# Hybrid decoder block on one core: earlier decay rows and a narrower join in the DeltaNet solve

## The chip, the cores and the metric

The kernel runs on one core of a Trainium2 chip. The metric is the device time of one execution in microseconds, as the median of three runs. The core has TensorE (PE; its weight loads are listed as PEld), VectorE (DVE), ScalarE (ACT), GpSimd (POOL) and SyncE (SP), which here issues nearly all transfers from one queue, in order.

## The reference

One layer over 4096 tokens of width 1024, all in float32:

```python
h = rms_norm(x, attn_norm)
proj = h @ w_in                       # q, k, v, gate, beta, alpha of group A; q, k, v, gate of group B
o_a = gated_delta_net(...)            # 4 heads of 128, chunked WY form, decay exp(cumsum(g))
o_b = retention(...)                  # 4 heads of 128, rotary phase, fixed decay per head
x = x + concat(o_a, o_b) @ w_out
x = x + hierarchical_moe(rms_norm(x, ffn_norm), ...)   # 64 experts, top group, top 2
return rms_norm(x, final_norm)
```

The change touches `gated_delta_net` alone. For each chunk it forms a strictly lower triangular matrix from k, beta and the decay, and solves a unit triangular system with it:

```python
a_mat = where(strict, (kb @ k.T) * decay, 0)
uw = triangular_solve(a_mat, [v*beta, kb*exp(gc)], lower=True, unit_diagonal=True)
```

## The kernel before

The mixer (both attention groups) takes tokens in eight blocks of 512 and chunks of 128. A block has four stages in the order a1, b1, a0, b0: `a` projects for two DeltaNet heads (a *pair*), `b` for two retention heads. A stage `a` has four "normal" projections (`proj_n`, L244 to L246; 128 tokens by 256 columns, 24 matmuls) for the gates and three groups of two "transposed" ones (`proj_t`, L232 to L234) for q, k and v; a stage `b` has sixteen normal ones. Each matrix is split into a high and a low part, hence three matmuls per step. The results go into one of two accumulators in PSUM (`pacc`), and a projection can't start before the one two back has been emptied: by L846 and L849 (rotary phase, VectorE), L861 (ScalarE) or L277 and L279 (gates).

Everything else is laid between the projections by hand. After each projection, and in the middle of each transposed one, `unit` is called. It first issues the stores that are due, then runs the steps that `STEPS` lists: `W` asks for the four weight tiles of the next group (`wq`, 512 KB each, only at the group's first unit), `E` empties the accumulator, `L` advances the DeltaNet chain of the pair, and so on. A group of four units counts `u` from 0 to 3. The chain `gdn_pair` is a generator: `PLAN[pr]` says how many of its steps each unit runs. It is started at the end of a stage `a` and runs through the following stages `b` and `a`. In each block the pair `pr` = 1 comes first (called the first pair here), `pr` = 0 second.

The steps of `gdn_pair` that matter here:

- At its start it asks for `E` (L641): for each of two heads the running decays of 512 tokens, repeated over 128 partitions, read from `gcd` in DRAM, which L380 wrote during the first projection pair of stage a1. Then come transposes and norms; `decay` (L653 to L658) makes the decay matrix from `E`: an exponential on ScalarE, a product on GpSimd, four operations on VectorE, another exponential.
- L696 to L704 form the matrices `at` and `am`. L711 and L712 take the diagonal 32-blocks, a constant pattern is loaded into `V` (L686), and L722 to L732 solve the 32-blocks on VectorE. L736 clears `X2`; L739 and L756 turn the result back.
- The join of 32-blocks into 64-blocks: `mask` (L749) multiplies `at` by a 0/1 mask on GpSimd, for each head; L784 multiplies the masked matrix with `X`, ScalarE copies all 512 columns (L785), L791 multiplies with `U`, VectorE adds (L792).
- The join of 64-blocks into 128 (L765 to L778) works on 64 by 64 pieces.
- L801 to L826 run over the chunks; each ends in `norm_out`, which leaves a store of `mx` (two buffers) to `mixed` in the list of stores (L296).

After the mixer come the output projection, the routing and the experts, which the change leaves alone.

Of the kernel before, what the change touches and what calls it, by code (L numbers as in the profile page):

```python
# [8 lines left out]
F32 = mybir.dt.float32  # L9
# [3 lines left out]
AF = mybir.ActivationFunctionType  # L13
OP = mybir.AluOpType
# [3 lines left out]
P = 128  # L18
# [3 lines left out]
NT = T // P  # L22
# [4 lines left out]
GA, BA = 1536, 2048  # L27
QB, KB, VB, GB = 2056, 2568, 3080, 3592
NEXP, NGRP, EPG, DE = 64, 8, 8, 256
LEVELS = (32, 64)  # L30
B = LEVELS[0]
NB = P // B
NQ = P // (2 * NB * NT)

C_UT, C_NEG, C_LV = 0, 128, 256
C_CV = C_LV + 128 * len(LEVELS)
C_EF = C_CV + 4
C_ID = C_EF + 4
C_ROW = C_ID + P
# [3 lines left out]
def constants(S):  # L43
    i = np.arange(P)
    J, I = np.meshgrid(i, i, indexing="ij")
    c = np.zeros((P, C_N), np.float64)
    c[:, C_ID:C_ID + P] = J == I
    c[:, C_UT:C_UT + P] = I >= J
    c[:, C_ROW:] = (I[:, :B // NQ, None] * NQ + J[:, :B // NQ, None] % B // (2 * NT) == i[:B]).reshape(P, -1)
    c[:, C_NEG:C_NEG + P] = np.where(I >= J, 0.0, -1e4)  # L50
    for n, m in enumerate(LEVELS):
        c[:, C_LV + n * P:C_LV + (n + 1) * P] = (
            (J // (2 * m) == I // (2 * m)) & ((J // m) % 2 == 0) & ((I // m) % 2 == 1))
    for h in range(4):
        g = 1.0 - 2.0 ** (-5.0 - h)
        c[:, C_CV + h] = DK ** -0.5 * g ** -(i + 1.0)
        c[:, C_EF + h] = EPS * g ** (-2.0 * (i + 1.0))
    pos = np.arange(S, dtype=np.float32)
    inv = (np.float32(10000.0) ** (-np.arange(0, DK, 2, dtype=np.float32) / np.float32(DK))).astype(np.float32)
    ang = (pos[:, None] * inv[None, :]).astype(np.float32).astype(np.float64)  # L60
    co, si = np.cos(ang), np.sin(ang)
    rope = np.concatenate([co, -si, si], axis=1).astype(np.float32)
    return c.astype(np.float32), rope


def rows(ap, off, pat):
    return bass.AP(tensor=ap.tensor, offset=ap.offset + off, ap=pat)
# [6 lines left out]
def mixer(tc, outer, banks, x, attn_norm, w_in, conv_a, a_log, dt_bias, norm_a, norm_b, cst, rope, mixed, clear, w_out, x1, wsp):  # L74


    nc = tc.nc
# [3 lines left out]
    pacc, ptr, psm = (pool(tc, banks, n, b, space=PSUM) for n, b in (("pa", 2), ("pt", 3), ("ps", 3)))  # L81
    wp, hp, xp = (pool(tc, outer, n, 1) for n in "whx")
    with ExitStack() as ctx:
        cp, gp, sp = (pool(tc, ctx, n, b, side="right") for n, b in (("c", 1), ("g", 2), ("s", 2)))
# [4 lines left out]
        C = cp.tile([P, C_ID], F32, name="cst")  # L89
        ident = wp.tile([P, P], F32, name="id")  # L90
# [102 lines left out]
        la, lb = Lane(), Lane()  # L193
        late, bg, stores = [], [], []
# [7 lines left out]
            if bg:  # L202
                bg.pop(0)()

        def store():
            due, stores[:] = stores[:], []
            for f in due:
                f()

# [1 line left out]

        def unit(u, evac, kind):

            store()
            g = gi[0]
            act = dict(L=la.tick, E=evac or (lambda: None), T=later, S=lambda: ahead(4 * g + 5, u, False),
                       W=lambda: ahead(4 * g + 5, u, True), B=behind)
            for o in STEPS[kind]:
                act[o]()
            if u == 3:  # L220
                gi[0] += 1

        def w(k):
            m = 4 * gi[0] + k // 2
# [58 lines left out]
        def norm_out(po, e, gs, t0, col):  # L283
            ss = sp.tile([P, 2], F32, name="ss", bufs=4)
            jk = sp.tile([P, P], BF, name="jk", bufs=2)
            for i in range(2):
                nc.scalar.activation(jk, po[:, i], AF.Square, accum_out=ss[:, i:i + 1])
            nc.vector.scalar_tensor_tensor(ss, ss, 1.0 / P, e, op0=OP.mult, op1=OP.add)  # L288
            nc.gpsimd.tensor_tensor(ss, ss, ex[:, 0:2], op=OP.pow)  # L289
            m = sp.tile([P, 2, P], F32, name="mx", bufs=2)  # L290

            def rest():
                for i in range(2):
                    nc.vector.scalar_tensor_tensor(m[:, i], po[:, i], ss[:, i:i + 1], gs[:, i * P:i * P + P],
                                                   op0=OP.mult, op1=OP.mult)
                stores.append(lambda: nc.sync.dma_start(mixed[t0:t0 + P, col:col + 256], m.rearrange("p a b -> p (a b)")))  # L296
            return rest
# [40 lines left out]
        def decays(ba):  # L338
# [41 lines left out]
            nc.sync.dma_start(gcd, gr)  # L380
            yield gcd

        L = dict(locals())
        with tc.manual_schedule():
            x_load(0)
# [41 lines left out]
            for sb in range(NS):  # L427
# [4 lines left out]
                for kind, pr in stages:  # L432
# [3 lines left out]
                    if kind == "a":  # L436

                        n = 264 if pr else 256
                        gs = []
                        if pr:  # L440
                            ba = gp.tile([P, NT, 8], F32, name="ba")
                        for i in range(NT):
# [4 lines left out]
                            a = proj_n(i, n)  # L447
# [6 lines left out]
                        if pr:  # L454
                            dec = decays(ba)
                            co = next(dec)
                            bg += [lambda: next(dec)] + [lambda: None] * 1 + [lambda: next(dec), lambda: box.append(next(dec))]
                            box = []


                        dst, ready = [], []
                        for wi in range(3):
                            dst.append(gp.tile([P, 2, T], F32, name="qkv"[wi] + "t", bufs=(1, 2, 1)[wi]))
                            for cc in range(2):
                                ch = wi * 4 + 2 * pr + cc
                                a = proj_t(cc)
                                unit(2 * cc + 1, lambda: take(a, ch, dst[wi][:, cc], ready), "t")
                        la.start(gdn_pair(tc, sb, pr, co, box[0], gs, dst, ready, L), PLAN[pr])
                    else:
                        if last and pr and sb:  # L470
                            out.begin()
# [149 lines left out]
                      zt[:, None, :].to_broadcast([P, m, ZW]))  # L621


def gdn_pair(tc, sb, pr, co, gcd, gs, qkv, ready, L):
    nc = tc.nc
    sp, gp, ptr, psm, ex, Sa = L["sp"], L["gp"], L["ptr"], L["psm"], L["ex"], L["Sa"]
    ident, neg, C, norm_out = L["ident"], L["neg"], L["C"], L["norm_out"]
# [7 lines left out]
    vr = gp.tile([P, 2, NT, P], F32, name="vr", bufs=1)  # L635
    jk = sp.tile([P, P], BF, name="jk", bufs=2)
    tkc = lambda w, i, c: tk[:, w, 4 * i + c:4 * i + c + 1]
    E, qd = [], []
    for i, h in enumerate(hs):
        e = gp.tile([P, NT, P], F32, name="E", bufs=2)  # L640
        nc.sync.dma_start(e, rows(gcd, h * P, [[0, P], [4 * P, NT], [1, P]]))  # L641
        E.append(e)

    def turn(src):
        tr = ptr.tile([P, NT, P], F32, name="tr")
# [35 lines left out]
    at, am = [], []  # L681
    blocks = [(slice(b * B, b * B + B), b) for b in range(NB)]
    at2, N = (gp.tile([P, 2 * NT, P], F32, name=n, bufs=1) for n in ("at", "U"))
    N = N.rearrange("p a b -> p (a b)").rearrange("p (r s) -> p r s", r=B)
    V = sp.tile([P, B // NQ, B], F32, name="V", bufs=1)
    nc.sync.dma_start(V.rearrange("p r s -> p (r s)"), L["cst"][:, C_ROW:])  # L686
    for i, h in enumerate(hs):
        a_ = at2[:, i * NT:i * NT + NT]
        m_ = gp.tile([P, NT, P], F32, name="am")
# [47 lines left out]
    yield  # L737
    for sl, b in blocks:
        nc.vector.transpose(X2[sl, :, sl].rearrange("p c (r q) -> p r q c", q=NQ), V[sl])  # L739
    U, X = ([t[:, :NT], t[:, NT:]] for t in (U2, X2))  # L740
    flat = lambda t: t.rearrange("p a b -> p (a b)")
    mts = {}

    def mask(li):
        lv = C[:, C_LV + li * P:C_LV + li * P + P][:, None, :].to_broadcast([P, NT, P])
        mts[li] = []
        for i in range(2):
            mt = gp.tile([P, NT, P], F32, name="E", bufs=2)
            nc.gpsimd.tensor_tensor(mt, at[i], lv, op=OP.mult)  # L749
            mts[li].append(mt)  # L750

    mask(0)
    yield

    for i in range(2):
        nc.vector.transpose(flat(U[i]), flat(X[i]))  # L756
    yield
    for li, m in enumerate(LEVELS):
        if m == 64:

            a, b = slice(0, 64), slice(64, P)
            for i in range(2):
                tr = ptr.tile([P, NT, P], F32, name="tr")
                for c in range(NT):
                    nc.tensor.transpose(tr[a, c, a], U[i][a, c, a], ident[a, a])  # L765
                nc.scalar.activation(X[i][a, :, a], tr[a, :, a], AF.Copy)
            yield
            for i in range(2):
                w = psm.tile([P, NT, P], F32, name="sm")
                for c in range(NT):  # L770
                    nc.tensor.matmul(w[b, c, a], at[i][a, c, b], X[i][a, c, a], start=True, stop=True)
                nc.scalar.activation(X[i][b, :, a], w[b, :, a], AF.Copy)
            yield
            for i in range(2):
                pu = psm.tile([P, NT, P], F32, name="sm")
                for c in range(NT):
                    nc.tensor.matmul(pu[a, c, b], X[i][b, c, a], U[i][b, c, b], start=True, stop=True)
                nc.vector.tensor_tensor(U[i][a, :, b], U[i][a, :, b], pu[a, :, b], op=OP.add)  # L778
            yield
            continue  # L780
        for i in range(2):
            w = psm.tile([P, NT, P], F32, name="sm")
            for c in range(NT):
                nc.tensor.matmul(w[:, c], mts[li][i][:, c], X[i][:, c], start=True, stop=True)  # L784
            nc.scalar.activation(X[i], w, AF.Copy)  # L785
        yield
        r = s = slice(0, P)
        for i in range(2):
            pu = psm.tile([P, NT, P], F32, name="sm")
            for c in range(NT):  # L790
                nc.tensor.matmul(pu[r, c, s], X[i][:, c, r], U[i][:, c, s], start=True, stop=True)  # L791
            nc.vector.tensor_tensor(U[i][r, :, s], U[i][r, :, s], pu[r, :, s], op=OP.add)  # L792
        yield


    rest = None
# [1014 lines left out]
```

## Time and profile before

| what | us |
|---|---|
| median of three runs | 3616.17 (3609.36 to 3617.98) |
| the profiled execution | 3614.18 |
| its span, first to last instruction | 3612.4 |
| TensorE busy in it | 3405.1 (94%) |
| VectorE, ScalarE, GpSimd busy | 2206.6, 1500.5, 1052.1 |

The profile lists instructions by their line in the kernel. "Idle before" is the time an engine stood before an instruction, with what ended the wait; "issue" is time in which it waited for nothing that the profile shows. A matmul of float32 operands is two instructions. The granted clock (PEclk) is the share of TensorE's full 2.4 GHz; 0.50 is 1.2 GHz.

### The profile page before, as it was taken

What the parts mean: (1) busy time and instruction counts of PE and PEld (TensorE: products, weight loads), DVE (VectorE), ACT (ScalarE), POOL (GpSimd) and SP (SyncE); (2) the same over time, 40 slices, a digit from 0 to 9 for tenths busy, and PEclk for the clock granted to TensorE, in tenths of its full rate; (3) what the DMA queues carried; (4) which work ended last, traced back from release to release, by engine and by line L of the source; (5) the groups of instructions that cost most, each with busy time, mean ns of one, the idle gap of its engine ahead of it and who ended that gap; (6) DMA issues with size and microseconds to landing.
All of it is one profiled execution on the core that took longest, in us unless ns stands there. A gap on an engine that the chain in (4) does not pass through costs nothing. (4 is left out here: it accounts for less than half of the span.)

```text
span 3612.4 us, 65017 instructions
## 1 busy us (share of the span) xinstructions
PE 3405.1 (94%) x24177; PEld 3118.7 (86%) x24177; DVE 2206.6 (61%) x5766; ACT 1500.5 (42%) x3322; POOL 1052.1 (29%) x1352
## 2 busy tenths in 40 slices
PE   7999999999999999999999999999969999999996
PEld 6988988988998998989899898888858888888885
DVE  6785565575576566466466564444456777777775
ACT  4343233233233333323323332222136666776775
POOL 1322222232232232232222220211223444444443
PEclk9999999999999999999999999999979999999998
DMA  8766346445455355364444435332268898899996
GB/s 269 239 209 216 125 144 208 147 145 189 147 158 191 127 173 187 140 187 162 159 146 172 161 110 168 115 121 97 78 198 287 286 307 291 304 327 331 342 317 194
DMA packets 463375, 711.10 MB, mean 197 GB/s; under 512 B 151329, under 2 KB 342353, under 8 KB 463057
## 3 DMA queue, kind: packets, MB, share of 16 engines
q1 hardware_dynamic: 426688, 622.16, 51.9%
q0 software_dynamic: 34976, 84.20, 6.6%
q8 instruction: 191, 3.13, 0.3%
q14 instruction: 128, 1.04, 0.1%
q10 hardware_dynamic: 1392, 0.56, 0.1%
HBM read 606.32 MB, written 131.99 MB: 204 GB/s over the span
## 5 line engine op out<-in xcount | busy, mean ns | idle before, releaser
L244 PE MATMUL acc<-wq,hh 128*128 128x256 f32 (+1 forms) x2560 | 760.1, 297 | 92.8 <-issue 51.4
L245 PE MATMUL acc<-wq,hh 128*128 128x256 f32 (+1 forms) x2560 | 733.5, 287 | 1.9 <-DVE wq L150 1.9
L246 PE MATMUL acc<-wq,hl 128*128 128x256 f32 (+1 forms) x2560 | 733.0, 286 | 2.1 <-DVE hl L324 2.1
L244 PEld LDWEIGHTS acc<-wq,hh 128*128 128x128 f32 x2560 | 495.6, 194 | 104.4 <-issue 63.9
L245 PEld LDWEIGHTS acc<-wq,hh 128*128 128x128 f32 x2560 | 496.7, 194 | 2.4 <-DVE wq L150 2.4
L246 PEld LDWEIGHTS acc<-wq,hl 128*128 128x128 f32 x2560 | 495.1, 193 | 2.8 <-DVE hl L324 2.8
L232 PE MATMUL acc<-hh,wq 128*128 128x512 f32 x768 | 317.8, 414 | 0.5 <-DMA wq<-wsp 0.3
L234 PE MATMUL acc<-hh,wq 128*128 128x512 f32 x768 | 302.1, 393 | 0.0
L233 PE MATMUL acc<-hl,wq 128*128 128x512 f32 x768 | 300.9, 392 | 0.0
L1622 PEld LDWEIGHTS g<-xT,gu 128*128 128x128 f32 x2048 | 273.3, 193 | 15.0 <-DVE xT L1554 5.4
L1622 PE MATMUL g<-xT,gu 128*128 128x128 f32 (+30 forms) x2048 | 279.0, 295 | 2.7 <-DVE xT L1554 2.7
L1622 PE MATMUL u<-xT,gu 128*128 128x128 f32 (+30 forms) x2048 | 275.9, 293 | 0.0
L1622 PEld LDWEIGHTS u<-xT,gu 128*128 128x128 f32 x2048 | 266.3, 191 | 1.9
L272 DVE SCALAR_TENSOR_TENSOR cv<-xin,pcol,cv 128x512 f32<-128x512 f32 x288 | 216.3, 751 | 73.3 <-ACT cv L270 66.5
L280 POOL TENSOR_TENSOR gs<-gs,nrow 128x256 f32<-128x256 f32 x128 | 97.4, 761 | 512.6 <-DVE gs L279 486.9
L850 POOL TENSOR_TENSOR rqk<-rqk,rb 128x256 f32<-128x256 f32 x128 | 116.1, 908 | 250.8 <-DVE rb L849 178.3
L1597 POOL DMA_INDIRECT out_dram<-xg,mi x100 | 131.8, 1318 | 188.0 <-DVE ss L1593 95.9
L976 PE MATMUL y<-dh,hh 128*128 128x512 f32 (+16 forms) x400 | 164.7, 412 | 20.5 <-ACT ys L1565 12.8
L1565 ACT ACTIVATE ys<-y,mf 128x512 f32<-128x512 f32 (+22 forms) x200 | 133.6, 679 | 114.2 <-PE y L978 95.6
L1568 POOL DMA_INDIRECT xg<-out_dram,mi x97 | 100.3, 1034 | 251.6 <-PE tr L1552 45.3
L234 PEld LDWEIGHTS acc<-hh,wq 128*128 128x128 f32 x768 | 144.2, 188 | 32.9
L289 POOL TENSOR_TENSOR ss<-ss,ex 128x2 f32<-128x2 f32 x128 | 101.7, 795 | 238.3 <-DVE ss L288 205.2
(376 smaller groups left out, 8007.1 us busy)
## 6 DMA issues: line engine op xcount, KB each, us to landing
wq<-wsp SPq DMA_DIRECT2D x420, 512.0 KB
gu<-in_w_gate_dram SPq DMA_DIRECT2D x128, 512.0 KB
gu<-in_w_up_dram SPq DMA_DIRECT2D x128, 512.0 KB
dn<-in_w_down_dram SPq DMA_DIRECT2D x64, 1024.0 KB
xi<-in_x_dram SPq DMA_DIRECT2D x64, 512.0 KB
wsp<-wq SPq DMA_DIRECT2D x60, 512.0 KB
mixed<-mx SPq DMA_DIRECT2D x128, 128.0 KB
out_dram<-zt SPq DMA_DIRECT2D x8, 2048.0 KB
```

The source lines that it names most:

```text
L232: nc.tensor.matmul(a, wh[:, s], hh[:, k, :], start=(k == 0), stop=False)
L233: nc.tensor.matmul(a, wh[:, s], hl[:, k, :], start=False, stop=False)
L234: nc.tensor.matmul(a, wl[:, s], hh[:, k, :], start=False, stop=(k == KC - 1))
L244: nc.tensor.matmul(a[:, :n], hh[:, k, s], wh[:, :n], start=(k == 0), stop=False)
L245: nc.tensor.matmul(a[:, :n], hh[:, k, s], wl[:, :n], start=False, stop=False)
L246: nc.tensor.matmul(a[:, :n], hl[:, k, s], wh[:, :n], start=False, stop=(k == KC - 1))
L272: nc.vector.scalar_tensor_tensor(cv, xin[:, j:j + T], tap(j), cv, op0=OP.mult, op1=OP.add)
L850: nc.gpsimd.tensor_tensor(o.rearrange("p h s d -> p (h s d)"), o.rearrange("p h s d -> p (h s d)"), b.rearrange("p h s d -> p (h s d)"), o ...
L976: nc.tensor.matmul(out, a.hi, b.hi, start=(i == 0), stop=False)
L1565: nc.scalar.activation(self.y[:R, s], y[:R], AF.Copy, scale=self.f[:R, WT, self.n:self.n + 1])
L1597: so = nc.gpsimd.indirect_dma_start(out=orow, out_offset=self.idx(0), in_=self.xg[:self.G], in_offset=None, bounds_check=S - 1, oob_is_err ...
L1622: nc.tensor.matmul(o[:, b, :R], self.w.gu[k // 4][:, k % 4, i * DE + b * P:i * DE + b * P + P], self.xT[:, k, :R], start=(k == 0), stop=(k ...
```

## The change

Three edits, in the functions shown above.

- The request for `E` and `V` moves from the chain into a new function `preload`, which stage `a` calls before the third pair of transposed projections (`wi` = 2). `E` is no longer used for masks.
- The join of 32-blocks multiplies without masks, and with 64 moving columns in place of 128; all eight chunks of a pair of heads go into one PSUM tile. The rows that matter are copied (ScalarE, 32 rows by 256 columns, two copies) in place of whole tiles and in place of additions on VectorE. In the 64-join the two heads share a PSUM tile and a copy. The number of steps of the chain is the same.
- In a group's first three units the stores that are due are issued after the unit's steps, and so behind the weight loads; in the fourth they stay in front. `mx` has three buffers.

```diff
-        def store():
-            due, stores[:] = stores[:], []
+        def store(n=None):
+            due, stores[:n] = stores[:n], []
...
-            store()
+            due = len(stores)
+            if u == 3:
+                store()
...
             if u == 3:
                 gi[0] += 1
+            else:
+                store(due)
...
-            m = sp.tile([P, 2, P], F32, name="mx", bufs=2)
+            m = sp.tile([P, 2, P], F32, name="mx", bufs=3)
...
+        def preload(pr, gcd):
+
+            E = []
+            for h in (2 * pr, 2 * pr + 1):
+                e = gp.tile([P, NT, P], F32, name="E", bufs=2)
+                nc.sync.dma_start(e, rows(gcd, h * P, [[0, P], [4 * P, NT], [1, P]]))
+                E.append(e)
+            V = sp.tile([P, B // NQ, B], F32, name="V", bufs=1)
+            nc.sync.dma_start(V.rearrange("p r s -> p (r s)"), cst[:, C_ROW:])
+            return E, V
...
                             for cc in range(2):
+                                if wi == 2 and cc == 0:
+                                    first = preload(pr, box[0])
                                 ch = wi * 4 + 2 * pr + cc
...
-                        la.start(gdn_pair(tc, sb, pr, co, box[0], gs, dst, ready, L), PLAN[pr])
+                        la.start(gdn_pair(tc, sb, pr, co, first, gs, dst, ready, L), PLAN[pr])
...
-    mask(0)
-    yield
-
-    for i in range(2):
-        nc.vector.transpose(flat(U[i]), flat(X[i]))
-    yield
...
-        for i in range(2):
-            w = psm.tile([P, NT, P], F32, name="sm")
-            for c in range(NT):
-                nc.tensor.matmul(w[:, c], mts[li][i][:, c], X[i][:, c], start=True, stop=True)
-            nc.scalar.activation(X[i], w, AF.Copy)
-        yield
-        r = s = slice(0, P)
-        for i in range(2):
-            pu = psm.tile([P, NT, P], F32, name="sm")
-            for c in range(NT):
-                nc.tensor.matmul(pu[r, c, s], X[i][:, c, r], U[i][:, c, s], start=True, stop=True)
-            nc.vector.tensor_tensor(U[i][r, :, s], U[i][r, :, s], pu[r, :, s], op=OP.add)
-        yield
+    U = [U2[:, :NT], U2[:, NT:]]
+    yield
+
+    for t in range(2):
+        h = slice(t * NT, t * NT + NT)
+        nc.vector.transpose(U2[:, h].rearrange("p a b -> p (a b)"), X2[:, h].rearrange("p a b -> p (a b)"))
+    yield
+    even, odd = (lambda t, c, o=o: t[:, c].rearrange("p (m o s) -> p m o s", o=2, s=B)[:, :, o] for o in range(2))
+    w = psm.tile([P, 2 * NT, 2 * B], F32, name="sm")
+    for c in range(2 * NT):
+        nc.tensor.matmul(w[:, c], at2[:, c], even(X2, c), start=True, stop=True)
+    for m in range(2):
+        r = slice((2 * m + 1) * B, (2 * m + 2) * B)
+        nc.scalar.activation(X2[r, :, 2 * m * B:2 * m * B + B], w[r, :, m * B:m * B + B], AF.Copy)
+    yield
+    pu = psm.tile([P, 2 * NT, 2 * B], F32, name="sm")
+    for c in range(2 * NT):
+        nc.tensor.matmul(pu[:, c], X2[:, c], odd(U2, c), start=True, stop=True)
+    for m in range(2):
+        r = slice(2 * m * B, 2 * m * B + B)
+        nc.scalar.activation(U2[r, :, (2 * m + 1) * B:(2 * m + 2) * B], pu[r, :, m * B:m * B + B], AF.Copy)
+    yield
+    a, b = slice(0, 64), slice(64, P)
+    tr = ptr.tile([P, 2 * NT, 64], F32, name="tr")
+    for c in range(2 * NT):
+        nc.tensor.transpose(tr[a, c], U2[a, c, a], ident[a, a])
+    nc.scalar.activation(X2[a, :, a], tr[a], AF.Copy)
+    yield
...
+        nc.tensor.matmul(pu[a, c], X2[b, c, a], U2[b, c, b], start=True, stop=True)
+    nc.vector.tensor_copy(U2[a, :, b], pu[a])
+    yield
```

## Rows read from the trace of the kernel before

**Rows 1.** Busy time by stretch: us; PE, PEld, DVE, ACT, POOL; PEclk, DMA share, GB/s.
```profile
1060.00:1145.00 85.00, 85.00 (x605) 77.94 (x604) 46.08 (x122) 34.25 (x112) 18.41 (x35) 1.00 0.63 200
0.00:2135.00 2135.00, 2022.00 (x14845) 1900.47 (x14846) 1325.27 (x3658) 740.51 (x2207) 567.46 (x836) 0.98 0.52 172
```

**Rows 2.** Groups by line and shape, TensorE, mixer: busy us, mean ns; idle before.
```profile
L244 PE MATMUL acc<-wq,hh 128*128 128x256 f32 x2304 | 681.9, 296 | 90.4 <-issue 51.4 <-DVE gs L279 21.6 <-DVE rb L849 13.5
...
L232 PE MATMUL acc<-hh,wq 128*128 128x512 f32 x768 | 317.8, 414 | 0.5 <-DMA wq<-wsp 0.3
```

**Rows 3.** Waits, whole span: who waited for whom, us, times, longest.
```profile
DVE E L657 <- ACT qd L653: 81.3, 16, 6.6
...
ACT qd L653 <- DMA E<-gcd: 58.0, 14, 5.0
```

**Rows 4.** Timeline of a second pair, 1005 to 1053 us: start, duration, engine, line.
```profile
1009.46 0.63 ACT L653 ACTIVATE qd<-E 128x512 f32<-128x512 f32 x1 [3.77 <-DMA E<-gcd]
...
1013.95 0.48 DVE L849 TENSOR_TENSOR rb<-acc,rt 128x128 f32<-128x128 f32 x2
...
1014.53 0.36 PE L244 MATMUL acc<-wq,hh 128*128 128x256 f32 x1 [3.30 <-issue]
...
1027.56 0.36 PE L244 MATMUL acc<-wq,hh 128*128 128x256 f32 x1 [0.93 <-DVE rb L849]
...
1052.82 0.58 PE L244 MATMUL acc<-wq,hh 128*128 128x256 f32 x1 [2.46 <-DVE gs L279]
```

**Rows 5.** Busy time by stretch, after the two stalls of that pair.
```profile
1015.20:1018.60 3.40, 3.40 (x18) 3.40 (x17) 3.40 (x7) 0.00 (x0) 3.02 (x4) 0.50 0.04 7
...
1052.90:1056.30 3.40, 3.40 (x17) 3.40 (x18) 1.90 (x4) 1.32 (x3) 1.41 (x2) 0.52 0.03 12
1056.40:1059.80 3.40, 3.40 (x32) 3.40 (x31) 0.92 (x3) 1.43 (x6) 1.38 (x3) 1.00 0.00 0
```

**Rows 6.** Timeline of SP's queue before a first pair, 1115 to 1140 us.
```profile
1115.73 0.32 SPq L296 DMA_DIRECT2D mixed<-mx  x1
1116.14 1.82 SPq L143 DMA_DIRECT2D wq<-wsp  x4
1125.70 10.85 SPq L296 DMA_DIRECT2D mixed<-mx  x2
1136.67 2.08 SPq L143 DMA_DIRECT2D wq<-wsp  x4
1138.85 1.15 SPq L641 DMA_DIRECT2D E<-gcd  x2
```

**Rows 7.** Busy time by stretch, around that request; DMA share and GB/s last.
```profile
1124.00:1136.00 12.00, 12.00 (x83) 10.99 (x82) 7.86 (x17) 5.33 (x16) 2.09 (x4) 1.00 0.03 11
1138.00:1148.00 10.00, 9.62 (x84) 9.43 (x82) 1.93 (x5) 4.39 (x20) 1.11 (x2) 1.00 0.96 334
```

**Rows 8.** Timelines of VectorE and GpSimd: the 32-block solve and the masks.
```profile
240.00 5.00 DVE L726 SCALAR_TENSOR_TENSOR V<-U,V 128x31 f32<-128x31 f32 x12
...
1033.74 2.60 POOL L749 TENSOR_TENSOR E<-at,cst 128x512 f32<-128x512 f32 x2
...
1168.22 2.59 DVE L726 SCALAR_TENSOR_TENSOR V<-U,V 128x31 f32<-128x31 f32 x12
...
2085.64 5.10 DVE L726 SCALAR_TENSOR_TENSOR V<-U,V 128x31 f32<-128x31 f32 x12
```

**Rows 9.** Timelines of TensorE and its weight loads: joins and two narrow matmuls.
```profile
1072.82 1.95 PE L791 MATMUL sm<-U,X 128*128 128x128 f32 x16
...
1083.45 1.14 PE L771 MATMUL sm<-X,at 64*64 64x64 f32 x16
...
1099.45 0.30 PEld L366 LDWEIGHTS sm<-co,cst 128*128 128x128 f32 x2
1099.67 0.30 PEld L367 LDWEIGHTS sm<-co,cst 128*128 128x128 f32 x2
```

**Rows 10.** Groups by line and shape, ScalarE, mixer.
```profile
L711 ACT ACTIVATE X<-at 32x256 f32<-32x256 f32 x64 | 26.6, 415 | 30.1 <-DVE at L702 29.6
```

More of the change, by code (lines that the diff above doesn't have):

```diff
@@ L29 @@
 NEXP, NGRP, EPG, DE = 64, 8, 8, 256
-LEVELS = (32, 64)
-B = LEVELS[0]
+B = 32
 NB = P // B
 NQ = P // (2 * NB * NT)
-C_UT, C_NEG, C_LV = 0, 128, 256
-C_CV = C_LV + 128 * len(LEVELS)
+C_UT, C_NEG, C_CV = 0, 128, 256
 C_EF = C_CV + 4
@@ L50, in constants @@
     c[:, C_NEG:C_NEG + P] = np.where(I >= J, 0.0, -1e4)
-    for n, m in enumerate(LEVELS):
-        c[:, C_LV + n * P:C_LV + (n + 1) * P] = (
-            (J // (2 * m) == I // (2 * m)) & ((J // m) % 2 == 0) & ((I // m) % 2 == 1))
     for h in range(4):
@@ L621, in zero, with gdn_pair @@
                       zt[:, None, :].to_broadcast([P, m, ZW]))
-def gdn_pair(tc, sb, pr, co, gcd, gs, qkv, ready, L):
+def gdn_pair(tc, sb, pr, co, first, gs, qkv, ready, L):
     nc = tc.nc
@@ L637, in gdn_pair @@
     tkc = lambda w, i, c: tk[:, w, 4 * i + c:4 * i + c + 1]
[L638 to L642, printed above, removed]
+    (E, V), qd = first, []
     def turn(src):
@@ L684, in gdn_pair @@
     N = N.rearrange("p a b -> p (a b)").rearrange("p (r s) -> p r s", r=B)
-    V = sp.tile([P, B // NQ, B], F32, name="V", bufs=1)
-    nc.sync.dma_start(V.rearrange("p r s -> p (r s)"), L["cst"][:, C_ROW:])
     for i, h in enumerate(hs):
@@ L739, in gdn_pair @@
         nc.vector.transpose(X2[sl, :, sl].rearrange("p c (r q) -> p r q c", q=NQ), V[sl])
[L740 to L746, printed above, removed]
-        for i in range(2):
-            mt = gp.tile([P, NT, P], F32, name="E", bufs=2)
-            nc.gpsimd.tensor_tensor(mt, at[i], lv, op=OP.mult)
-            mts[li].append(mt)
@@ L752, in gdn_pair @@
-    mask(0)
+    U = [U2[:, :NT], U2[:, NT:]]
     yield
-    for i in range(2):
-        nc.vector.transpose(flat(U[i]), flat(X[i]))
+    for t in range(2):
+        h = slice(t * NT, t * NT + NT)
+        nc.vector.transpose(U2[:, h].rearrange("p a b -> p (a b)"), X2[:, h].rearrange("p a b -> p (a b)"))
     yield
-    for li, m in enumerate(LEVELS):
-        if m == 64:
-            a, b = slice(0, 64), slice(64, P)
-            for i in range(2):
-                tr = ptr.tile([P, NT, P], F32, name="tr")
-                for c in range(NT):
-                    nc.tensor.transpose(tr[a, c, a], U[i][a, c, a], ident[a, a])
-                nc.scalar.activation(X[i][a, :, a], tr[a, :, a], AF.Copy)
-            yield
-            for i in range(2):
-                w = psm.tile([P, NT, P], F32, name="sm")
-                for c in range(NT):
-                    nc.tensor.matmul(w[b, c, a], at[i][a, c, b], X[i][a, c, a], start=True, stop=True)
-                nc.scalar.activation(X[i][b, :, a], w[b, :, a], AF.Copy)
-            yield
-            for i in range(2):
-                pu = psm.tile([P, NT, P], F32, name="sm")
-                for c in range(NT):
-                    nc.tensor.matmul(pu[a, c, b], X[i][b, c, a], U[i][b, c, b], start=True, stop=True)
-                nc.vector.tensor_tensor(U[i][a, :, b], U[i][a, :, b], pu[a, :, b], op=OP.add)
-            yield
[L780 to L783, printed above, removed]
-                nc.tensor.matmul(w[:, c], mts[li][i][:, c], X[i][:, c], start=True, stop=True)
-            nc.scalar.activation(X[i], w, AF.Copy)
-        yield
-        r = s = slice(0, P)
-        for i in range(2):
-            pu = psm.tile([P, NT, P], F32, name="sm")
-            for c in range(NT):
-                nc.tensor.matmul(pu[r, c, s], X[i][:, c, r], U[i][:, c, s], start=True, stop=True)
-            nc.vector.tensor_tensor(U[i][r, :, s], U[i][r, :, s], pu[r, :, s], op=OP.add)
-        yield
@@ L796, in gdn_pair @@
+    yield
+    w = psm.tile([P, 2 * NT, 64], F32, name="sm")
+    for c in range(2 * NT):
+        nc.tensor.matmul(w[b, c], at2[a, c, b], X2[a, c, a], start=True, stop=True)
+    nc.scalar.activation(X2[b, :, a], w[b], AF.Copy)
+    yield
+    pu = psm.tile([P, 2 * NT, 64], F32, name="sm")
+    for c in range(2 * NT):
+        nc.tensor.matmul(pu[a, c], X2[b, c, a], U2[b, c, b], start=True, stop=True)
+    nc.vector.tensor_copy(U2[a, :, b], pu[a])
+    yield
     rest = None
```

## The prediction

> **What bounds the kernel now.** I read the stretch table first. In the mixer (0 to 2135 us) TensorE is busy 2022 us [rows 1], so 113 us of idle time is there to be had, and in a stretch that nothing disturbs, 1060 to 1145 us, it has no gap at all. The mixer's end is therefore set by TensorE: work on another engine costs time only where it makes TensorE stand, and the question is what makes it stand.
>
> The groups by line answer most of that: 90.4 us of the gap stand before one line, the first matmul of a normal projection (L244); 51.4 us are put down to "issue", 21.6 us to L279 (gate, VectorE), 13.5 us to L849 (rotary phase, VectorE) [rows 2]. "Issue" names nothing, so I went to the list of waits: ScalarE's L653 waits 58.0 us in 14 times, at most 5.0, for the DMA of the decay rows `E`, and VectorE's L657 waits 81.3 us for L653 [rows 3].
>
> The timeline of one pair (the second of its 512-token block, 1005 to 1053 us) ties them together [rows 4]. L653 starts at 1009.46 after 3.77 us of waiting for `E`. VectorE works in order and stands at L657 for it, and behind L657 stand L846 and L849, which empty the projection's PSUM; L849 starts at 1013.95. TensorE has two accumulators; it has been idle since 1011.2 and starts the next projection only at 1014.53, after L849's two operations: "issue" is that wait for L849. VectorE now carries a backlog, and TensorE meets it twice more: 0.93 us at 1027.56 (L849 again) and 2.46 us at 1052.82 (L279).
>
> The clock adds to it. After the 3.3 us stall the granted clock reads 0.50 (1.2 GHz) for 3.4 us, and after the stall at 1052.8 it reads 0.52; a stretch soon after reads 1.00 [rows 5]. In the slow 3.4 us 17 or 18 matmuls start, in the fast one 32, so some 1.5 us are lost each time.
>
> **The change part by part.**
>
> *Decay rows earlier.* Why `E` is late is in the queue of transfers: in the next pair four 512 KB weight loads are issued at 1136.67, `E` behind them at 1138.85, and the DMA engines are 0.96 busy from 1138 to 1148, with ScalarE released only then; from 1124 to 1136 they were 0.03 busy [rows 6, 7]. The change issues `E` (2 x 256 KB) and `V` (128 KB) after the second projection pair, in front of the four loads that went out at 1116.14: some 23 us sooner, against waits of at most 5.0 us [rows 3]. The write of the running decays, which `E` reads, is issued four units before that. Its buffers are free (their last reader is in the previous pair's start), as is that of `V`.
>
> What goes: the 14 waits, 58.0 us [rows 3]. Does VectorE's gain reach TensorE in full? In the pair shown, L657 can start 3.77 us sooner and everything behind it moves along, since VectorE was packed; the stall of 3.30 us goes, TensorE gets ahead, and it next meets VectorE at 1027.56, which is 3.8 us earlier too. So the stall and the slow clock together (3.3 + 1.5 us) are paid back as 3.8 us, the amount of the `E` wait. What is late next is that L849: TensorE gets there 3.3 + 1.5 + 0.9 = 5.7 us sooner, VectorE 3.8, so some 2 us of waiting stay. In a first pair the same reckoning gives its own `E` wait (up to 5.0 us). Term: **58 us**. The ends: 51 us if only the "issue" stalls go; 68 us if in first pairs, where no second stall follows, some of the slow clock (7 x 1.5 us) is regained too.
>
> What stands behind the three transfers in SP's queue: the four weight loads move back by three issues (under 2 us, with two of `E` at 1.15 us) and by 640 KB (1.9 us at the 334 GB/s of the busy stretch). The DMA engines were idle from 1124 to 1136 [rows 6, 7], so they have about 12 us in hand; cost 0, and if that cover is gone, see the rivals.
>
> *The masks go.* Two GpSimd multiplications of 1.3 us per pair. In second pairs they start at 1033.74, amid VectorE's 12 operations of L726, which take 5.00 us (240.00, the first) to 5.10 us (2085.64, the last) in the eight of these pairs; in a first pair the masks run after the solve, and the same 12 take 2.59 us [rows 8]. So the overlap costs VectorE 2.4 us in eight pairs, inside the backlog that TensorE meets at L279 (21.6 us, 2.7 us a pair [rows 2]). The stall is as long as the saving, so it comes through: 8 x 2.4 = 19 us; I take **17 us**, because a short GpSimd operation also falls into that stretch and stays. Ends: 0 (VectorE is held by something else) and 19.
> With the stall down to some 0.3 us, the slow clock after it (1.5 us, [rows 5]) should not come: 8 x 1.5 = **12 us**, ends 0 and 12.
>
> *Half the columns in the join.* 32 batches (16 pairs, two each) of 8 matmuls, two instructions each: 512 instructions. With 128 moving columns 16 of them take 1.95 us, 0.12 us each. The trace has none with 128 stationary and 64 moving columns. The nearest above is L366/L367, with 128 stationary and only 16 moving columns: their weight loads start at 1099.45 and 1099.67 with two instructions each, so still 0.11 us for one. The nearest below is the 64x64 join, 16 in 1.14 us or 0.07 us each, but its stationary side is 64 wide as well [rows 9]. So 0 to 512 x 0.05 = 26 us; I take **0**, by L366, which shares the stationary width that stays at 128.
> The Trainium skill speaks against this part of the change: "TensorE: Matmul & The Clock Gate", section LDWEIGHTS, has the load's time go with the stationary operand's columns (by its formula an estimate of 107 ns for 128), not with what is streamed. The 0.11 us of L366 agrees, and by it the sum gets nothing here. The same page's section "Back-to-back issue gap" has an isolated spacing of N/2.4 + 2.5 ns; if that ruled, nearly half of the 0.12 us would go, at most 31 us.
>
> *The other edits of the join.* ScalarE: two 128x512 copies become two of 32x256 (0.415 each by L711 [rows 10]), two more such copies come in place of two VectorE additions; pairs of small copies become one. All of it lies where TensorE never waits [rows 1], as do the merged additions; without that cover each is worth under 1 us a pair. Cost 0.
> *Stores behind the weight loads, a third `mx`.* SP alone waits in this queue, and TensorE waits 0.3 us in all for those loads (L232 [rows 2]). Nobody reads `mixed` before the mixer's end. Cost 0; without the cover, the 0.32 us of one issue per store [rows 6].
>
> Sum: 58 + 17 + 12 + 0 = 87 us. The profiled execution took 3614.2 us (span 3612.4), so 3527; the median of the runs is 2 us above it: **3529 us**.
>
> **The rivals.**
> A. *Narrower matmuls do run faster.* For it: 64-wide joins at 0.07 us. Against it: L366 [rows 9]. 3529 - 26 = 3503 us. (The page's second section above would have it so or a little better.)
> B. *Only the `E` wait pays.* VectorE's backlog of second pairs is held by another step, or the slow clock comes back after the 2 us stall that is left at L849; then 17 + 12 go missing: 3558 us. For it: a stall of 2.46 us was followed by a clock of 0.52 [rows 4, 5], and that is little more than 2. Against it: VectorE's operations behind L657 follow each other in a fixed order, and what is taken from among them moves all the rest.
> C. *The request is not earlier in effect.* SP issues in order, and a store of `mx` in front of `E` waits for VectorE; such stores held the queue from 1125.70 to 1136.55 [rows 6]. If one like it stands in front of `E`, nothing moves but the masks: 3616 - 17 - 12 = 3587, or 3616 with the masks hidden too. Against it: the store in front is that of 1115.73, and even a request at 1126 would find idle DMA engines.
> D. *Slower: weights late.* `E` and `V` push four weight loads back, and TensorE stands at the first rotary projection of every pair. It decides from 12 us of delay; to eat the 87 us and 11 more over 14 pairs it needs 7 us of standing each, 19 us of delay in all, against the 4 us reckoned above. From there on the time is over 3627 us.
>
> **How the numbers follow.** Chances: forecast 0.67, A 0.09, B 0.15, C 0.06, D 0.03. The range 3500 to 3562 takes in A, B and the ends of the first term, and leaves out C and D. A difference under 0.3% (11 us) can't be told from no change; C splits over faster and the same: faster 0.93, same 0.04, slower 0.03.
>
> **What would show it.** Right: no wait of L653 for `E`; no "issue" before L244; L726's twelve at 2.6 to 3.0 us in every pair; L279's share of L244's idle time under 5 us; clock 1.00 where [rows 5] has 0.5; 128x64 joins at 0.11 to 0.12 us each. Wrong: L232 or L244 waiting for `wq` (D); `E` issued behind a long store (C); L849 taking the stalls over with the clock at 0.5 (B); joins near 0.07 us each (A).

## The result and the profile after

The changed kernel takes 3527.6 us (median of four runs, 3525.5 to 3531.7), 0.9765 of the kernel before (95% interval 0.9746 to 0.9784, 3612.8 us in the same comparison). The forecast was 3529. A total can come out right for wrong reasons, so the terms are looked at one by one: first in the profile after, then by runs of one part each. Line numbers shift from kernel to kernel; L243 is the old L244, L278 the old L279, L661 and L665 the old L653 and L657, L839 the old L849, L732 the old L726.

Busy time by stretch of the changed kernel: the mixer up to about its last join, and 3.4 us after a stall of a second pair (columns as in [rows 1]).

```profile
0.00:2046.00 2046.00, 1989.72 (x14843) 1870.32 (x14844) 1284.44 (x3611) 742.34 (x2207) 526.29 (x804) 1.00 0.55 179
...
1015.60:1019.00 3.40, 3.40 (x30) 3.40 (x31) 1.97 (x4) 2.33 (x6) 1.48 (x2) 1.00 0.47 154
```

The group by line and shape that carried the stalls [rows 2]:

```profile
L243 PE MATMUL acc<-wq,hh 128*128 128x256 f32 x2304 | 672.0, 292 | 36.1 <-DVE rb L839 23.5 <-DVE gs L278 6.7 <-DVE st L311 4.0
...
L231 PE MATMUL acc<-hh,wq 128*128 128x512 f32 x768 | 317.7, 414 | 0.4 <-DMA wq<-wsp 0.4
```

"Issue" is gone from it, L278 fell from 21.6 to 6.7 us, and L839 rose from 13.5 to 23.5: TensorE stands 90.4 - 36.1 = 54 us less here. The rest is clock: the mean granted clock of the whole run went from 0.978 to 0.986.

```profile
core 0: 3529.9 us, clock 0.986
```

The stretch tables show what both are worth in the mixer. TensorE is idle there for 56 us where it was idle for 113, and busy for 1990 us where it was busy for 2022 with as many matmuls to within two ([rows 1] against the row above): 57 + 32 = 89 us, of which the narrower join makes under 2 (see below). Between the two spans lie only 82.5 us, so behind the mixer, which the change leaves alone, this execution took some 6 us longer. From the last projection to the end the profiled executions of this document take 1491 to 1499 us, and this one takes the longest.

The timeline of the second pair that [rows 4] shows, now at 974 to 1016 us:

```profile
974.41 0.62 ACT L661 ACTIVATE qd<-E 128x512 f32<-128x512 f32 x1
...
975.06 2.27 DVE L665 SCALAR_TENSOR_TENSOR E<-E,co,cst 128x128 f32<-128x128 f32 x4 [1.43 <-ACT qd L661]
...
992.41 0.36 PE L243 MATMUL acc<-wq,hh 128*128 128x256 f32 x1 [1.56 <-DVE rb L839]
...
1015.58 0.39 PE L243 MATMUL acc<-wq,hh 128*128 128x256 f32 x1 [0.40 <-DVE gs L278]
```

L661 follows the work before it without a wait. Of the three stalls the first is gone, the second is 1.56 us where some 2 were expected, the third 0.40 where 0.3 were, and the clock behind it reads 1.00 (above). First pairs have a stall before L243 as well. Behind neither kind does the clock fall; one stretch of each is shown, and all fourteen between 366 and 2000 us read 1.00:

```profile
1119.85 0.35 PE L243 MATMUL acc<-wq,hh 128*128 128x256 f32 x1 [1.32 <-DVE rb L839]
...
992.40:995.80 3.40, 3.16 (x25) 3.00 (x26) 3.30 (x7) 0.00 (x0) 1.77 (x2) 1.00 0.42 133
1119.90:1123.30 3.40, 3.40 (x29) 3.40 (x30) 1.68 (x6) 0.00 (x0) 1.35 (x2) 1.00 0.45 133
```

The queue of transfers shows the request in front of the loads, before the second pair above and before a first pair [rows 6], and with it ScalarE's first use of `E` in that first pair:

```profile
937.02 11.36 SPq L295 DMA_DIRECT2D mixed<-mx  x2
948.47 1.00 SPq L387 DMA_DIRECT2D E<-gcd  x2
...
1070.92 6.18 SPq L295 DMA_DIRECT2D mixed<-mx  x2
1077.21 0.99 SPq L387 DMA_DIRECT2D E<-gcd  x2
1078.25 0.50 SPq L390 DMA_DIRECT2D V<-in_cst_dram  x1
1078.84 2.14 SPq L138 DMA_DIRECT2D wq<-wsp  x4
...
1103.03 0.62 ACT L661 ACTIVATE qd<-E 128x512 f32<-128x512 f32 x1
```

In both, two stores of `mx` stand right in front of the request and hold the queue, for 11.4 and 6.2 us. It still goes out 26 us before L661 in either pair (948.47 and 974.41, 1077.21 and 1103.03).

And the solve [rows 8], with what GpSimd does beside it in the second pair:

```profile
996.84 2.89 DVE L732 SCALAR_TENSOR_TENSOR V<-U,V 128x31 f32<-128x31 f32 x12
...
997.00 0.74 POOL L840 TENSOR_TENSOR rqk<-rqk,rb 128x256 f32<-128x256 f32 x1 [0.58 <-DVE rb L839]
997.69 0.95 POOL L742 MEMSET X<- 128x1024 f32 x1
...
1124.30 2.59 DVE L732 SCALAR_TENSOR_TENSOR V<-U,V 128x31 f32<-128x31 f32 x12
```

It takes 2.89 us in second pairs, where it took 5.0, and 2.59 us in first ones, as before.

### The profile page after: what moved, and what is told of

It is laid out like the page before. It is cut to its first block, busy times and chain, and to the rows that moved or that the text cites. A ratio compares the mean times of both kernels' runs of the same rounds, so it can differ in the third digit from the quotient of the medians.

```text
span 3529.9 us, 64890 instructions
## 1 busy us (share of the span) xinstructions
PE 3373.2 (96%) x24177; PEld 3090.6 (88%) x24177; DVE 2166.1 (61%) x5718; ACT 1502.5 (43%) x3322; POOL 1012.8 (29%) x1320
## 5 line engine op out<-in xcount | busy, mean ns | idle before, releaser
L243 PE MATMUL acc<-wq,hh 128*128 128x256 f32 (+1 forms) x2560 | 751.1, 293 | 38.5 <-DVE rb L839 23.5
L245 PE MATMUL acc<-wq,hl 128*128 128x256 f32 (+1 forms) x2560 | 724.1, 283 | 2.1 <-DVE hl L323 2.1
L244 PE MATMUL acc<-wq,hh 128*128 128x256 f32 (+1 forms) x2560 | 724.6, 283 | 0.2 <-DVE wq L145 0.2
L243 PEld LDWEIGHTS acc<-wq,hh 128*128 128x128 f32 x2560 | 487.5, 190 | 49.3 <-issue 26.5
L245 PEld LDWEIGHTS acc<-wq,hl 128*128 128x128 f32 x2560 | 485.8, 190 | 2.8 <-DVE hl L323 2.8
L244 PEld LDWEIGHTS acc<-wq,hh 128*128 128x128 f32 x2560 | 487.4, 190 | 0.6 <-DVE wq L145 0.5
L231 PE MATMUL acc<-hh,wq 128*128 128x512 f32 x768 | 317.7, 414 | 0.4 <-DMA wq<-wsp 0.4
L279 POOL TENSOR_TENSOR gs<-gs,nrow 128x256 f32<-128x256 f32 x128 | 97.0, 758 | 543.6 <-DVE gs L278 517.5
L840 POOL TENSOR_TENSOR rqk<-rqk,rb 128x256 f32<-128x256 f32 x128 | 115.8, 905 | 250.6 <-DVE rb L839 178.9
```

Source lines behind the costliest of these rows:

```text
L231: nc.tensor.matmul(a, wh[:, s], hh[:, k, :], start=(k == 0), stop=False)
L243: nc.tensor.matmul(a[:, :n], hh[:, k, s], wh[:, :n], start=(k == 0), stop=False)
L244: nc.tensor.matmul(a[:, :n], hh[:, k, s], wl[:, :n], start=False, stop=False)
L245: nc.tensor.matmul(a[:, :n], hl[:, k, s], wh[:, :n], start=False, stop=(k == KC - 1))
L840: nc.gpsimd.tensor_tensor(o.rearrange("p h s d -> p (h s d)"), o.rearrange("p h s d -> p (h s d)"), b.rearrange("p h s d -> p (h s d)"), o ...
```

## The experiments

Ratios are to the kernel before, run on the same chip, with 95% intervals.

### One part alone

**early_request_only**: the kernel before with `preload` and its call, masks and wide join kept.

```diff
+                                if wi == 2 and cc == 0:
+                                    first = preload(pr, box[0])
...
-        nc.sync.dma_start(e, rows(gcd, h * P, [[0, P], [4 * P, NT], [1, P]]))
...
-    nc.sync.dma_start(V.rearrange("p r s -> p (r s)"), L["cst"][:, C_ROW:])
```

> The kernel before with the early request for E and V alone (masks, 128-column join and the order of stores as before). The sum's theory: the 14 waits for E go, worth 58 us, so 0.984 of before (3555 us), L653 no longer waits, and L279 still makes TensorE stand some 2.4 us or more in second pairs with slow clock behind it. Rival 1, the early request carries the whole gain: 0.976. Rival 2, the masks and the clock carry it and the request is hidden: 1.00.

Measured: 0.9832 (0.9818 to 0.9845), 61 us less. The group by line and shape:

```profile
L244 PE MATMUL acc<-wq,hh 128*128 128x256 f32 x2304 | 673.4, 292 | 50.5 <-DVE rb L856 23.3 <-DVE gs L279 21.5 <-DVE st L312 3.9
```

The "issue" stalls are gone and no wait for `E` is left in the list of waits; the 21.5 us before L279 stand as before, and L856 (the old L849) has taken 10 us more. `V` moves along with `E` in this run, but the waits of the kernel before hold none for `V`. So the first term stands on its own: 61 us against 58, and the stall that goes is partly given back at the rotary phase, as reckoned.

**join_only**: the kernel before with the new join, `E` asked for at the chain's start and the stores as before.

```diff
-    mask(0)
...
+        nc.tensor.matmul(w[:, c], at2[:, c], even(X2, c), start=True, stop=True)
...
+        nc.tensor.matmul(pu[:, c], X2[:, c], odd(U2, c), start=True, stop=True)
```

> The kernel before with the new join alone (no masks, 64 moving columns, copies on ScalarE; E asked for at the chain's start, stores as before). The sum's theory: 17 us from VectorE in second pairs and 12 us of slow clock, so 0.992 (3584 us), L726's twelve operations at 2.6 to 2.9 us in every pair, the issue stalls and the waits for E all still there. Rival, the narrower matmuls count: 26 us more, 0.985. Rival, the backlog of second pairs is held by something else: 1.00.

Measured: 0.9935 (0.9921 to 0.9948), 23 us less (interval 19 to 29); the sum had 29. The group of the first matmul, the wait for `E`, and the stretch behind the "issue" stall of a first pair:

```profile
L239 PE MATMUL acc<-wq,hh 128*128 128x256 f32 x2304 | 682.0, 296 | 74.1 <-issue 52.4 <-DVE rb L828 12.3 <-DVE gs L274 6.6
```

```profile
ACT qd L648 <- DMA E<-gcd: 59.0, 14, 4.9
```

```profile
618.30:621.70 3.40, 3.40 (x21) 3.40 (x22) 3.40 (x9) 0.00 (x0) 2.56 (x3) 0.71 0.24 90
```

Here the picture is the other way round: "issue" and the wait for `E` are untouched, and the stalls of the gate (L274 here) fall from 21.6 to 6.6 us, 15 us less. The clock gives less than the 12 us of the sum: three "issue" stalls behind which it read 1.00 in the kernel before (at 624, 750 and 1416 us) are followed by 0.71, 0.68 and 0.52 here. The two parts add up: 61 + 23 = 84 us, against 85 for the whole change.

### What in the join made the gain

**masks_back**: the changed kernel with two GpSimd products per pair where the masks were made. They multiply `at` by the identity and nothing reads them: work is added and nothing else changed. They write to the `E` buffers, as the masks did, and no wait for `E` comes of it.

```diff
+    for i in range(2):
+        mt = gp.tile([P, NT, P], F32, name="E", bufs=2)
+        nc.gpsimd.tensor_tensor(mt, at[i], ident[:, None, :].to_broadcast([P, NT, P]), op=OP.mult)
```

> The changed kernel with two GpSimd products of 128x512 per pair at the place where the masks were made; they multiply the same matrix by the identity, and nobody reads the result. The sum's theory: GpSimd's operations hold VectorE in the solve of second pairs, so the solve takes 5.0 us there again, L278's stall is back at 2.4 us with slow clock behind it, and the time is 29 us above the changed kernel: 0.984 of before (3557 us). Rival, the join's other edits made the gain: 0.976, unchanged.

Measured: 0.9828 (0.9814 to 0.9841), 23 us above the changed kernel (0.0063 of 3613). The solve of a second pair, two of its twelve operations by themselves, GpSimd beside them, and the stall that follows:

```profile
1007.57 5.01 DVE L732 SCALAR_TENSOR_TENSOR V<-U,V 128x31 f32<-128x31 f32 x12
```

```profile
1009.43 2.52 DVE L732 SCALAR_TENSOR_TENSOR V<-U,V 128x26 f32<-128x26 f32 x2
```

```profile
1008.40 0.95 POOL L742 MEMSET X<- 128x1024 f32 x1
1009.32 2.60 POOL L749 TENSOR_TENSOR E<-at,id 128x512 f32<-128x512 f32 x2
```

```profile
1028.38 0.39 PE L243 MATMUL acc<-wq,hh 128*128 128x256 f32 x1 [2.48 <-DVE gs L278]
```

GpSimd's two products alone, with no other edit taken back, put the solve at 5.0 us and the stall at 2.48 us again: within some 5 us the whole of the join's gain is what they cost VectorE. The run lies beside early_request_only (3551.3 and 3553.9 us), from which it differs in all the other edits: the narrower join, its copies, the stores and the third buffer.

The expected 29 us came to 23. The stalls before L278 grew by 14.8 us, from 6.7 to 21.5; how much the clock adds is seen in the stretches behind them, four of eight here:

```profile
520.60:524.00 3.40, 3.40 (x20) 3.40 (x21) 1.94 (x4) 1.90 (x4) 1.45 (x2) 0.66 0.06 24
774.90:778.30 3.40, 3.40 (x30) 3.40 (x30) 1.98 (x4) 2.32 (x6) 1.48 (x2) 1.00 0.09 36
1028.40:1031.80 3.40, 3.40 (x29) 3.40 (x30) 1.98 (x4) 2.31 (x6) 1.48 (x2) 1.00 0.07 27
1534.80:1538.20 3.40, 3.40 (x19) 3.40 (x20) 1.93 (x4) 1.55 (x4) 1.44 (x2) 0.60 0.06 22
```

They follow stalls of 2.48, 2.37, 2.48 and 2.43 us. Of all eight, four are followed by the slow clock and four are not, where the kernel before had it behind each of its eight (0.52 to 0.72). TensorE's own timeline behind the first of the four:

```profile
520.55 0.39 PE L243 MATMUL acc<-wq,hh 128*128 128x256 f32 x1 [2.48 <-DVE gs L278]
...
521.49 0.28 PE L244 MATMUL acc<-wq,hh 128*128 128x256 f32 x1
521.61 0.32 PE L245 MATMUL acc<-wq,hl 128*128 128x256 f32 x1
521.73 0.41 PE L243 MATMUL acc<-wq,hh 128*128 128x256 f32 x1
521.94 0.41 PE L244 MATMUL acc<-wq,hh 128*128 128x256 f32 x1
```

The starts lie 0.12 us apart at first and 0.21 us from 521.73 on: 1.2 us after the stall the clock fell from 2.4 to 1.2 GHz. Behind the stall of the same length at 1028.38 it did not, 1.00 over the whole stretch.

**join_128_columns**: the changed kernel with all 128 moving columns in the join of 32-blocks.

```diff
-    w = psm.tile([P, 2 * NT, 2 * B], F32, name="sm")
-    for c in range(2 * NT):
-        nc.tensor.matmul(w[:, c], at2[:, c], even(X2, c), start=True, stop=True)
...
+    for t in range(2):
+        h = slice(t * NT, t * NT + NT)
+        w = psm.tile([P, NT, P], F32, name="sm")
+        for c in range(NT):
+            nc.tensor.matmul(w[:, c], at2[:, t * NT + c], X2[:, t * NT + c], start=True, stop=True)
...
```

> The changed kernel with 128 moving columns in the join of 32-blocks (two PSUM tiles, one per head, and four copies of 32x128 where there were two of 32x256). The sum's theory: matmuls with 128 stationary columns take 0.11 to 0.12 us whatever they stream, so 0.976 to 0.977 of before (3528 to 3532 us). Rival A, the narrower matmuls run faster: 26 us more, 0.984 (3554 us).

Measured: 0.9755 (0.9741 to 0.9768), the same as the changed kernel. The two joins by line and shape (busy us, mean ns), first this run, then the changed kernel:

```profile
L767 PE MATMUL sm<-U,X 128*128 128x128 f32 x256 | 31.3, 275 | 0.7 <-DVE Sb L879 0.7
L758 PE MATMUL sm<-X,at 128*128 128x128 f32 x256 | 31.1, 275 | 0.0
```

```profile
L763 PE MATMUL sm<-U,X 128*128 128x64 f32 x256 | 30.4, 272 | 0.9 <-DVE Sb L875 0.9
L756 PE MATMUL sm<-X,at 128*128 128x64 f32 x256 | 30.3, 271 | 0.0
```

Half the columns make 256 instructions 0.8 to 0.9 us shorter, 1.7 us in both together, not 26. Rival A falls.

### Why the decay rows were late, and the stores

**request_at_start**: the changed kernel with the request two projections later, right before the chain starts, but still in front of the next four weight loads.

```diff
-                                if wi == 2 and cc == 0:
-                                    first = preload(pr, box[0])
...
+                        first = preload(pr, box[0])
                         la.start(gdn_pair(tc, sb, pr, co, first, gs, dst, ready, L), PLAN[pr])
```

> The changed kernel with E and V asked for after the last projection of stage a, right before the chain starts: two projections later than in the change, but still in front of the four weight loads of the next group, which the kernel before issued first. The theory that E was late because it stood behind those loads: the transfers find idle DMA engines, L661 waits little or not at all, and the time stays within 0.3% of the changed kernel (0.976 of before). Rival, the lead of two projections is what counts: most of the 58 us come back, 0.99.

Measured: 0.9769 (0.975 to 0.9789), the same as the changed kernel, with no wait for `E`. SP's queue before a first pair:

```profile
1090.22 0.32 SPq L295 DMA_DIRECT2D mixed<-mx  x1
1090.63 1.00 SPq L387 DMA_DIRECT2D E<-gcd  x2
1091.68 0.49 SPq L390 DMA_DIRECT2D V<-in_cst_dram  x1
1092.27 3.08 SPq L138 DMA_DIRECT2D wq<-wsp  x4
```

Two projections of lead aren't needed. Being in front of the 2 MB of weights, behind one store of 0.32 us, is enough.

**stores_as_before**: the changed kernel with the old order of stores and two `mx` buffers.

```diff
-            due = len(stores)
-            if u == 3:
-                store()
+            store()
...
-            m = sp.tile([P, 2, P], F32, name="mx", bufs=3)
+            m = sp.tile([P, 2, P], F32, name="mx", bufs=2)
```

> The changed kernel with the stores issued at the start of every unit and two mx buffers, as before the change. The sum's theory: worth nothing, 0.976 to 0.977. Rival, long stores in front of the weight loads and of the request hold SP's queue: E is late again in part of the pairs, 0.98 or more.

Measured: 0.9772 (0.9755 to 0.979), the same. With this order a store of 0.32 us stands in front of the request, and the long stores come behind the loads; it is the new order that puts them in front (937.02 and 1070.92 above). The time is the same either way:

```profile
951.05 0.99 SPq L383 DMA_DIRECT2D E<-gcd  x2
952.10 0.50 SPq L386 DMA_DIRECT2D V<-in_cst_dram  x1
952.69 1.92 SPq L138 DMA_DIRECT2D wq<-wsp  x4
960.69 10.87 SPq L291 DMA_DIRECT2D mixed<-mx  x2
```

### What is late next

**turn_one_unit_later**: the changed kernel with a step boundary between L717 and L718, and the following unit one step longer.

```diff
-PLAN = ['12122113121120011111111111111111', '12122012212111111111111111111111']
+PLAN = ['12122213121120011111111111111111', '12122112212111111111111111111111']
...
         nc.scalar.activation(dg[sl], at2[sl, :, sl], AF.Copy)
+    yield
     nc.vector.transpose(N.rearrange("p r s -> p s r"),
```

> The changed kernel with a step boundary between ScalarE's copies of the diagonal blocks (L717) and VectorE's transpose of them (L718), and one more step in the plan for the next unit, so that the projection's L836 and L839 go ahead of that transpose on VectorE. It goes at what the forecast named as late next, the L839 stalls of 1.2 to 1.6 us in every pair (23.5 us in all). If VectorE's order makes them: they shrink to half or less, and the time falls 10 to 20 us (0.972). If VectorE simply has too much work there: the stall turns up at a later line, 0.976.

Measured: 0.9704 (0.9686 to 0.9721), 22 us below the changed kernel.

```profile
L243 PE MATMUL acc<-wq,hh 128*128 128x256 f32 x2304 | 671.6, 291 | 17.8 <-DVE gs L278 7.6 <-DVE rb L840 5.5 <-DVE st L311 4.0
```

The stalls of the rotary phase (L840 here) fall from 23.5 to 5.5 us without turning up elsewhere. So order made them: VectorE's transpose, 1.4 us of waiting for ScalarE included, stood in front of the two operations that free an accumulator.

**turn_and_late_product**: the same, and GpSimd's product of q with the decay at the 64-join.

```diff
-        nc.gpsimd.tensor_tensor(q.rearrange("p a b -> p (a b)"), q.rearrange("p a b -> p (a b)"), qt[:, i], op=OP.mult)
...
+    for i in range(2):
+        q = qd[i].rearrange("p a b -> p (a b)")
+        nc.gpsimd.tensor_tensor(q, q, qt[:, i], op=OP.mult)
```

> The run before, and the product of q with the decay (GpSimd, L662) moved from the chain's start to the 64-join. There it no longer meets L665 on VectorE, whose four operations took 2.3 and 2.6 us where operations of that kind without GpSimd beside them take 0.34 each: about 1 us of VectorE per head, 2 us per pair. If the two engines hold each other up as in the solve: L665's four at 1.4 to 1.6 us, the stalls at L839 and L278 nearly gone, 0.967 to 0.970. If not: as the run before.

Measured: 0.9672 (0.9654 to 0.969), 3492.8 us, the fastest version here, 11 to 12 us (0.0032) below the run before it. The intervals of the two meet at their edges, but no execution of one overlaps the other's (3490 to 3496 us against 3503 to 3510), and the profile shows the cause:

```profile
959.14 1.14 DVE L664 SCALAR_TENSOR_TENSOR E<-E,co,cst 128x128 f32<-128x128 f32 x4 [1.43 <-ACT qd L661]
...
965.08 1.61 DVE L664 SCALAR_TENSOR_TENSOR E<-E,co,cst 128x128 f32<-128x128 f32 x4
```

```profile
L243 PE MATMUL acc<-wq,hh 128*128 128x256 f32 x2304 | 671.4, 291 | 10.0 <-DVE gs L278 5.9 <-ACT wq L144 2.4 <-DVE rb L842 1.4
```

The four operations (L664 here) take 1.14 and 1.61 us for the two heads instead of 2.27 and 2.63, and the rotary stalls go down to 1.4 us. What is left before this line, 10 us, is a ninth of what the kernel before had.

## Why the prediction was right, point by point

- **The decay rows (58 us): right.** 61 us alone (interval 56 to 66). The reading that mattered was that neither the 51.4 us of "issue" nor the sum of stall and slow clock would come back, but the amount by which VectorE's queue moves up; L849's stalls grew from 13.5 to 23.5 us, which is that part given back. They stand in first pairs too (1.32 us at 1119.85), where the prediction saw no second stall; the detail was wrong and the term came out all the same. The cause in the transfer queue is confirmed by request_at_start: place, not lead.
- **The masks (17 us) and the slow clock behind them (12 us): right mechanism, 29 forecast, 23 measured** (interval 19 to 29, so the times alone hardly tell the two apart). L278's stalls fell by 14.9 us, of the 17. What is missing stands in the second pair of the first block, where the solve shortened like the others and the stall only went from 3.27 to 3.08 us; what else holds VectorE there stays open:

```profile
262.25 0.39 PE L243 MATMUL acc<-wq,hh 128*128 128x256 f32 x1 [3.08 <-DVE gs L278]
```

The larger part of the miss is the clock term. It counted one loss behind each of the eight stalls and took its upper end, 12 us, as the middle. In the kernel before each of the eight was indeed followed by the slow clock, but the losses don't come and go one by one with the stalls: put back alone, the masks bring four of the eight, and taken away alone they leave three new ones behind "issue" stalls.
- **Half the columns (0): right**, 1.7 us by the groups and nothing in the time.
- **Stores, third buffer, copies on ScalarE (0): right** for the stores and the buffer by their own run. The copies were not run alone; that masks_back and early_request_only take the same time leaves no room for more than some 5 us either way. One premise was wrong, at no cost that shows: `mixed` is read before the mixer's end, in the trace before from 1917 us on (L524).
- The total was nearer than its parts, and that is luck: the request brought 3 us more than its term and the masks and the clock 6 less.
- **The rivals.** A fell with join_128_columns. B fell: slow clock did not come back behind the 1.2 to 1.6 us that L839 holds (1.00 at 992.40 and 1119.90). C's sign came, without its effect: `E` is issued behind long stores (937.02, 1070.92), yet L661 never waits, since the request goes out 26 us before it is used. Of what the prediction held against C, the short store that it saw in front of the request was wrong; that a later request would still do was right, and request_at_start shows it too. D did not occur: TensorE waits 0.4 us in all for the weight loads of L231, where it was 0.3.
- **The other signs.** No wait for `E`, no "issue", the solve, the joins and the clock came as said. L278's share did not: 6.7 us where under 5 was named, 3.08 of it in the pair above.

## What to carry to other kernels

A stall whose releaser reads "issue" is worth following through the engine that empties the buffer: here the name of the culprit stood two engines and one transfer away, and its price was the shift of the queue in the middle, not the length of the stall. In a shared transfer queue look at what stands in front of a small urgent request before giving it more lead. A GpSimd product off the critical path was not free here where VectorE worked on SBUF operands at the same time: two of them made a 2.9 us solve a 5.0 us one. Moving one by a few units was worth 11 to 12 us, halving matmul columns nothing.

## What the runs showed of the hardware

- Two VectorE operations of 26 columns took 2.52 us beside two GpSimd products that took 2.60 (masks_back, 1009.43), so about as long as the products, while a 0.95 us GpSimd memset beside the same solve leaves it at 2.59 us in first pairs. The Trainium skill, "SBUF — State Buffer", section "Who interferes with whom", says that a VectorE instruction with two SBUF inputs contends with a GpSimd instruction that reads SBUF and not with one that only writes it, and calls such contention an exclusive lock. The traces agree: a product reads, a memset does not.
- Stalls of equal length, 2.48 us, were followed by either level of the clock (masks_back, 0.66 and 1.00). A stall's price in clock couldn't be read from its length alone.
- With 128 stationary columns the joins took 0.12 us per instruction with 64 moving columns as with 128 (30.4 and 31.3 us for 256).
